# RWKV-7 preparation in a hybrid decoder block: TensorE order written out, head sums as 64x64 products, bias one-hot loaded earlier

## The chip, the cores and the metric

One core of one Trainium2 chip. TensorE multiplies, VectorE and ScalarE do the elementwise work (ScalarE also the functions that need a table, such as Ln, Exp and Tanh), GpSimd (POOL in the profile) does a little of both, and SyncE, ScalarE and GpSimd issue DMAs. The metric is the device time of one execution in microseconds; several executions are given by their median.

## The reference

One decoder block on a sequence of 512 positions and 1024 channels, float32. The normed input is projected once; the columns go to a sparse-attention mixer (8 query heads, 2 key groups), an RWKV-7 mixer (8 heads of 64) and two gates. The two mixers are projected, gated, merged, projected again and added to the input; a gated MLP with a short convolution follows. The part that matters here is the preparation of the RWKV recurrence and the bias table of the attention:

```python
xl = p_in + (shifted - p_in) * mu
r, k, v, xw, xa, xg = jnp.split(xl, RWKV_SPLITS, axis=-1)
w = -jax.nn.softplus(-(w0 + jnp.tanh(xw) @ w2)) - 0.5
decay = jnp.exp(-jnp.exp(w.astype(jnp.float32)))
a = jax.nn.sigmoid(a0 + xa @ a2)
...
kk = k * k_k.reshape(H, N).astype(jnp.float32)
kk = kk / jnp.maximum(jnp.sqrt(jnp.sum(kk * kk, axis=-1, keepdims=True)), 1e-12)
k = k * (1.0 + (a - 1.0) * k_a.reshape(H, N).astype(jnp.float32))
...
y = y + jnp.sum(r * k * r_k, axis=-1, keepdims=True) * v
```

Two of these lines hold a sum over the 64 channels of each head: the norm of kk, and the bonus r * k * r_k.

## The kernel before, in words

Activations lie with channels on the 128 partitions and the 512 positions along the free dimension, so that one tile of 128x512 holds a *pair* of heads (64 partitions each). There are NH2 = 4 pairs. The weights are streamed as tiles of 128x1024 float32 (`raw`, 3 buffers); ScalarE rounds each to `whi` and VectorE (for a few tiles GpSimd) takes the rest `wlo` (line 296, 2 buffers each). The rounded input is `hh`, its rest `hl`. A *dense block* (`dense_fm`) is 24 products of 128x128 weights over 512 columns into one PSUM bank: for each of 8 k-tiles whi x hh and whi x hl, then 8 times wlo x hh.

PSUM has 8 banks, in three rings: `mm` with 4 banks, `a` with 2 and `b` with 2 (`mmb()`, `pa()`, `pb()`). A bank that is asked for again must first have been read by whoever reads its last contents.

The stage in question, lines 478 to 610, does for each pair p:

- `front(p)`: the dense block of the keys, two products of 64 rows with `wa` for decay and a (ring a and ring b), the shift mix of the keys (`shift_mix`, line 441: a copy with a scale on ScalarE, then a multiply-add on VectorE), two tanh, the cumulative sum over each chunk of 64 positions (`cum`, line 506), the exponentials `ep` and `pi`, and `PC` (line 513), the last decay of each chunk.
- `norms(p)`: the square of the keys, the *head sum* of it, that is a product with the block-diagonal 128x128 matrix `ones` (part of the tile `kc`) over 512 columns, then max (VectorE), Ln and Exp (ScalarE) into `rn`. Ln and Exp lie in different tables, so ScalarE loads a table ahead of each.
- `receptance(p)` and `values_of(p)`: a dense block and a shift mix each (`rx`, `vx`). `vx` has one buffer.
- `values_tok(p)`: four transposes of `vx` (line 542), copied to `UV` by ScalarE.
- `vectors(p)`: the elementwise products on VectorE that make `AR`, `kk`, `bh`, `aa`, `kx` and `tv`; at its end the head sum of `tv` and `BO`, the bonus.
- `gram(p)`: 16 transposes of `bh` (line 573, products of 64 rows, two at a time) into a bank of ring b and one of ring a, their copy `BKT` on ScalarE, then 16 products of 64x128 of `bh` with `AR`, the first half into rings b and a, the second into ring mm, and their masked copies `AB` on VectorE.

The loop stands at line 589. It names the steps in an order, but the order on each engine is the scheduler's. On TensorE it came out, for a steady pair, as: v block of p, k block of p + 1, the wa products, the value transposes of p, then the r block of p + 1 with the head sums of kk (p + 1) and tv (p) inside it, then transposes and products of the gram of p. So the small products of a pair lie in three places.

After the stage VectorE inverts 32x32 triangles (`inv`, memset on GpSimd at lines 620 and 621, transposes at 625 and 730) while TensorE runs the q block (`dense_tok`) and others, until `below` (line 740) needs the inverse. The bias table of the attention is one product of `rel_bias` (with a row of a large negative number) with a one-hot matrix. Both are loaded by ScalarE's DMA queue (lines 698 and 699) into a part of the tile `QK`; that part is also where the squares of q are written, so the loads come after these.

Of the kernel before, what the change touches and what calls it, by code (L numbers as in the profile page):

```python
# [25 lines left out]
NH2 = H // 2  # L26
# [54 lines left out]
def hybrid_block(ctx: ExitStack, tc: tile.TileContext, A: dict, out: bass.AP):  # L81
# [31 lines left out]
    def pa():  # L113
        return bank("a", 2)
# [376 lines left out]

    def front(p):
        cs = slice(128 * p, 128 * p + 128)
        kx = t2("kx", 2)
        pk = dense_fm(hh, hl)
        zw, za = pa(), pb()
        mm(zw, wa[0:64, cs], xw[0:64], True, True)
        mm(za, wa[64:128, cs], xw[64:128], True, True)
        shift_mix(pk, 4 + p, kx)
        cl = t2("cl")  # L500
# [12 lines left out]
        v.tensor_copy(PC[:, p, :, None], ep[:, :, C:C + 1])  # L513
        L[p] = dict(kx=kx, aa=aa, ep=ep, pi=pi)

    def norms(p):
        kx = L[p]["kx"]
        kk = t2("kk", 2)
        act(kk, kx, AF.Square, scale=col("rwkv_k_k", p))
        ss = pa()  # L520
        mm(ss, ones, kk, True, True)
        rn = t2("rn", 2)
        ts(rn, ss, 1e-24, None, op0=ALU.max)
        act(rn, rn, AF.Ln)
        act(rn, rn, AF.Exp, scale=-0.5)
        L[p].update(kk=kk, rn=rn)

# [20 lines left out]
    def vectors(p):  # L548
# [12 lines left out]
        stt(tv, rx, col("rwkv_r_k", p), kx, ALU.mult, ALU.mult)  # L561
        L[p]["bh"] = bh
        bs = pa()
        mm(bs, ones, tv, True, True)
        tt(BO[:, p], bs, vx, ALU.mult)

    def gram(p):
        bh = L[p]["bh"]
        ptr = [pb(), pa()]
        for c in range(NCH):  # L570
            for r in range(2):
                rs = slice(64 * r, 64 * r + 64)
                te.transpose(ptr[r][:, 64 * c:64 * c + 64], bh[rs, c, r:r + 2].rearrange("p a t -> p (a t)"),
                             ident[rs, rs])
        for r in range(2):
            act(BKT[:, :, p, r, :], ptr[r].rearrange("p (c j) -> p c j", c=NCH))
        for c0 in range(0, NCH, 4):
            ptr = [mmb(), mmb()] if c0 else [pb(), pa()]
            for i in range(4):
                for r in range(2):  # L580
                    rs = slice(64 * r, 64 * r + 64)
                    mm(ptr[r][:, 128 * i:128 * i + 128], bh[rs, c0 + i, r:r + 2].rearrange("p a t -> p (a t)"),
                       AR[rs, p, c0 + i].rearrange("p a t -> p (a t)"), True, True)
            for r in range(2):
                tt(AB[:, c0:c0 + 4, p, r, :], ptr[r].rearrange("p (c t) -> p c t", c=4),
                   mask[:, None, :].to_broadcast([128, 4, 128]), ALU.mult)


    front(0)
    norms(0)  # L590
    receptance(0)
    values_of(0)
    late_params()
    for p in range(NH2):
        if p + 1 < NH2:
            front(p + 1)
            norms(p + 1)
        values_tok(p)
        vectors(p)
        if p + 1 < NH2:  # L600
            receptance(p + 1)
        gram(p)
        if p + 1 < NH2:
            values_of(p + 1)
        if p + 2 == NH2:
            kcp = dense_fm(hh, hl)
    dbg("AR", AR)
# [72 lines left out]
    def windows(a, p):  # L680
        for g in range(2):
            for r in range(2):
                act(Dc[64 * r:64 * r + 64, a, g, :], p[64 * g:64 * g + 64, r::2])

    windows(0, kcp)
    urgent.append(1)
    bq = dense_tok(512, hh, hl)
    for t in range(NT):
        act(qn[:, t], bq[t])
        for h in range(H):  # L690
            act(QK[:, 2048 + 64 * h:2112 + 64 * h], bq[t][:, 64 * h:64 * h + 64], AF.Square,
                accum_out=qss[:, t, h:h + 1])
    windows(1, dense_fm(hh, hl))


    oh, rbx, vb = QK[0:33, 2048:2432], QK[0:33, 2440:2448], QK[0:8, 2560:2944]
    nc.gpsimd.memset(rbx[32:33], NEG)
    sc.dma_start(rbx[0:32], A["rel_bias"])
    sc.dma_start(oh, A["onehot"])
    pt = pa()  # L700
# [681 lines left out]
```

## Time and profile before

| | |
|---|---|
| median of 3 runs | 843.86 us (843.79 to 844.13) |
| the profiled execution's own time | 844.05 us |
| its span, first to last instruction | 842.3 us |
| mean granted TensorE clock | 1.0 |
| TensorE busy | 829.1 us, 98% |
| VectorE, ScalarE, GpSimd busy | 514.0, 405.9 and 52.4 us |

The page gives busy time by engine, then the span in slices, the DMA queues, the chain that ended last, and the groups of instructions. In a row of the timeline stand the start and the duration in us, the engine, the line, the operation, out<-in by tile name, the shape and the count; square brackets hold the idle time before it and who ended that. PE is TensorE, DVE is VectorE, ACT is ScalarE, POOL is GpSimd; q behind a name is the engine's own issuing of DMAs. TensorE's products are pipelined: the next starts before the row before has ended, so that the distance between starts is what one costs. The RWKV stage runs from about 27 to 123 us of the span.

### The profile page before, as it was taken

The page shows a single profiled execution, that of the slowest core. Times are in us where ns is not written, and L with a number is a line of the kernel's source. Part 1 is how long each engine was busy: PE and PEld are TensorE (multiplying, and loading weights), DVE is VectorE, ACT ScalarE, POOL GpSimd, SP SyncE. Part 2 cuts the span into 40 slices and gives each one's busy share as a digit, 9 for nine tenths or more (in the row PEclk, how much of TensorE's full clock was granted, in tenths as well). Part 3 has the DMA queues.
Part 4 walks back from the last instruction along what each step waited for, and adds up shares of the span by engine and source line. Part 5 has one row for each costly group of instructions (what it writes and reads, how often), then busy time and mean ns, then how long its engine had stood idle before and what let it go on. Part 6 is the DMA issues. An engine that isn't in the chain of part 4 may idle for free.

```text
span 842.3 us, 12845 instructions
## 1 busy us (share of the span) xinstructions
PE 829.1 (98%) x5097; PEld 674.3 (80%) x5097; DVE 514.0 (61%) x998; ACT 405.9 (48%) x784; POOL 52.4 (6%) x69
## 2 busy tenths in 40 slices
PE   7999999999999999999999999999999999999998
PEld 6777778887787886777788988888888888888886
DVE  5477779963556678888675576666556666322222
ACT  6766655452545677677344454444444444221210
POOL 6200020140000110111000000000000000000000
PEclk9999999999999999999999999999999999999999
DMA  7432222335461320010167033333333332223421
GB/s 228 115 82 68 75 75 76 92 104 156 126 126 51 88 63 13 22 31 26 51 204 234 0 99 90 90 97 100 100 100 100 96 90 93 98 100 113 138 75 51
DMA packets 109104, 78.73 MB, mean 93 GB/s; under 512 B 3869, under 2 KB 97748, under 8 KB 109044
## 3 DMA queue, kind: packets, MB, share of 16 engines
q1 hardware_dynamic: 106512, 73.51, 30.0%
q0 software_dynamic: 1472, 1.86, 1.0%
q10 hardware_dynamic: 1060, 2.55, 1.0%
q8 instruction: 40, 0.66, 0.3%
q14 instruction: 20, 0.16, 0.1%
HBM read 74.56 MB, written 2.29 MB: 91 GB/s over the span
## 4 chain that ended last, share of the span: by engine, by line
PE 53%; DVE 0%; DVEq 0%; issue 0%
PE ps_mm L120 52%; PE ps_b L203 0%; PE ps_a L203 0%; PE ps_a L120 0%; PE ps_b L1186 0%; PE ps_mm L1186 0%; DVE x L126 0%; DVEq L1378 0%; PE ps_a L1138 0%
## 5 line engine op out<-in xcount | busy, mean ns | idle before, releaser
L296 DVE TENSOR_TENSOR wlo<-raw,whi 128x1024 fp32r<-128x1024 f32 (+1 forms) x111 | 131.5, 1186 | 187.2 <-PE ps_mm L120 158.8
L120 PE MATMUL ps_mm<-hh,whi 128*128 128x512 f32 (+1 forms) x624 | 242.6, 391 | 0.0
L120 PE MATMUL ps_mm<-hl,whi 128*128 128x512 f32 (+1 forms) x624 | 240.4, 387 | 0.0
L123 ACT ACTIVATE whi<-raw 128x1024 fp32r<-128x1024 f32 (+3 forms) x124 | 123.3, 996 | 171.1 <-PE ps_mm L120 143.0
L120 PE MATMUL ps_mm<-hh,wlo 128*128 128x512 f32 (+1 forms) x624 | 151.8, 384 | 0.0
L120 PEld LDWEIGHTS ps_mm<-hh,whi 128*128 128x128 f32 x624 | 117.3, 188 | 26.7 <-issue 1.3
L120 PEld LDWEIGHTS ps_mm<-hl,whi 128*128 128x128 f32 x624 | 117.4, 188 | 23.5 <-issue 1.0
L120 PEld LDWEIGHTS ps_mm<-hh,wlo 128*128 128x128 f32 x624 | 115.1, 188 | 23.4
L120 PE MATMUL ps_mm<-whi,aT 128*128 128x512 f32 x352 | 84.5, 390 | 0.0
L120 PEld LDWEIGHTS ps_mm<-whi,aT 128*128 128x128 f32 x352 | 65.9, 188 | 14.3 <-issue 0.4
L135 DVE SCALAR_TENSOR_TENSOR cgv<-ps_mm,cw,cgv 128x511 f32<-128x511 f32 (+1 forms) x88 | 65.4, 746 | 1.6
L123 ACT ACTIVATE cgv<-ps_mm,cw 128x512 f32<-128x512 f32 x44 | 34.3, 781 | 23.3 <-PE ps_mm L120 23.3
L120 PE MATMUL ps_mm<-wlo,aT 128*128 128x512 f32 x176 | 44.3, 389 | 0.0
L123 ACT ACTIVATE P<-P,nm 128x512 f32<-128x512 f32 (+3 forms) x64 | 35.4, 553 | 14.9 <-DVE nm L1160 14.9
L123 ACT ACTIVATE aT<-cgv 128x512 fp32r<-128x512 f32 x22 | 13.9, 632 | 56.8 <-DVE cgv L126 56.8
L120 PEld LDWEIGHTS ps_mm<-wlo,aT 128*128 128x128 f32 x176 | 33.0, 188 | 6.9
L123 ACT ACTIVATE cgv<-cgv 128x512 f32<-128x512 f32 x22 | 13.9, 632 | 41.0 <-DVE cgv L135 41.0
L296 POOL TENSOR_TENSOR wlo<-raw,whi 128x512 fp32r<-128x512 f32 (+3 forms) x13 | 20.4, 1569 | 203.9 <-PE ps_mm L120 148.1
L1160 DVE CUSTOM_DVE_ANT_0 P<-ps_a,AB 128x512 f32<-128x512 f32 (+3 forms) x64 | 29.4, 484 | 4.2 <-PE ps_a L120 3.7
L126 DVE TENSOR_TENSOR x<-x,ps_mm 128x512 f32<-128x512 f32 (+1 forms) x17 | 11.0, 654 | 22.6 <-PE ps_mm L120 20.2
L126 DVE TENSOR_TENSOR aT<-cgv,aT 128x512 fp32r<-128x512 f32 x22 | 15.2, 693 | 14.7 <-ACT aT L123 14.7
L120 PE MATMUL ps_a<-KH,qst 128*128 128x512 f32 (+3 forms) x64 | 21.3, 348 | 1.5 <-DVE nm L1160 0.9
(356 smaller groups left out, 1201.7 us busy)
## 6 DMA issues: line engine op xcount, KB each, us to landing
raw<-in_w_up_dram SPq DMA_DIRECT2D x44, 512.0 KB, 3.8
raw<-in_w_in_dram SPq DMA_DIRECT2D x38, 512.0 KB, 3.9
raw<-in_w_down_dram SPq DMA_DIRECT2D x22, 512.0 KB, 3.6
raw<-in_w_out_dram SPq DMA_DIRECT2D x8, 512.0 KB, 3.9
xt<-in_x_dram SPq DMA_DIRECT2D x4, 512.0 KB, 5.8
raw<-in_cmp_w_k_dram SPq DMA_DIRECT2D x4, 512.0 KB, 4.4
raw<-in_cmp_w_v_dram SPq DMA_DIRECT2D x4, 512.0 KB, 4.4
raw<-in_w_proj_b_dram SPq DMA_DIRECT2D x8, 256.0 KB, 2.7
```

The lines of the kernel that those rows point to most:

```text
L120: te.matmul(o, lhsT=l, rhs=r, start=start, stop=stop)
L123: sc.activation(o, i, f, **kw)
L126: v.tensor_tensor(o, a, b, op=op)
L135: v.scalar_tensor_tensor(o, a, s, b, op0=op0, op1=op1)
L296: eng.tensor_tensor(lo, raw, hi.bitcast(F32), op=ALU.subtract)
L1160: v.tensor_tensor_reduce(out=P[:, i], in0=sp[:, N * (i - i0):N * (i - i0) + N], in1=BT[:, h, 384 - 128 * qt:512], scale=-1.0, scalar=-NEG, ...
```

## The change

- `front` is split: `keys_of` (k block, shift mix, square) and `decays` (wa products and what follows them).
- `head_sums` replaces each 128x128 product over 512 columns by four products of 64x64 weights over 256 columns: the first 256 columns by the two diagonal quarters into ring a, the other 256 by the two quarters off the diagonal into ring b, where the heads' results come out with their halves exchanged. What reads them (`EXCH`) works on one piece of 128x256 and two of 64x256; the max is in two pieces.
- The head sum of `tv` and `BO` move from the end of `vectors` to a step of their own, `bonus`, behind `gram`.
- `gram` puts its transposes into two banks of ring mm and its first products too, the second half into rings b and a (in the last pair the other way round); the copies to `BKT` have a high priority.
- TensorE's order is the written one for the whole stage: per pair the v block (at the end of the step before), the k block, the value transposes, the r block, then wa, head sum of kk, transposes and products of the gram, and the bonus sum in one stretch.
- The memset and the two loads for the bias table go to GpSimd's DMA queue, ahead of the q block; the squares of q are written in place in PSUM.

The scheduler still orders the other engines. In the changed program, for a steady pair, VectorE has: wlo of the next k block, mix of rx, the two max, cl, the scan, two AB, PC, AR, two AB, three BO, kk, AR, kk, bh, aa, the copy of bh, kx, wlo, mix of vx, the second part of bh, tv, wlo, mix of kx. ScalarE has: rx, the two tanh, a table load, Ln, two BKT, a table load, ep, pi, three Exp for rn, whi, vx, whi, kx, four UV, the square, whi. On GpSimd's queue the order is: the first memset of the inverse's tile, the bias memset, the load of rel_bias, the spare wlo (a part of the q weights that GpSimd splits), the second memset of the inverse's tile, the load of the one-hot.

```diff
--- before.py
+++ after.py
@@ -489,14 +489,18 @@
     L = {}
 
 
-    def front(p):
+    def keys_of(p):
+        kx = t2("kx", 2)
+        shift_mix(dense_fm(hh, hl), 4 + p, kx)
+        kk = t2("kk", 2)
+        act(kk, kx, AF.Square, scale=col("rwkv_k_k", p))
+        L.setdefault(p, {}).update(kx=kx, kk=kk)
+
+    def decays(p):
         cs = slice(128 * p, 128 * p + 128)
-        kx = t2("kx", 2)
-        pk = dense_fm(hh, hl)
         zw, za = pa(), pb()
         mm(zw, wa[0:64, cs], xw[0:64], True, True)
         mm(za, wa[64:128, cs], xw[64:128], True, True)
-        shift_mix(pk, 4 + p, kx)
         cl = t2("cl")
         act(cl, zw, AF.Tanh, scale=0.5, bias=w0h[:, p:p + 1])
         aa = t2("aa", 2)
@@ -511,19 +515,31 @@
         pi = t2("pi", 2)
         act(pi, cum, AF.Exp, scale=-1.0)
         v.tensor_copy(PC[:, p, :, None], ep[:, :, C:C + 1])
-        L[p] = dict(kx=kx, aa=aa, ep=ep, pi=pi)
+        L.setdefault(p, {}).update(aa=aa, ep=ep, pi=pi)
+
+
+
+    def head_sums(src):
+        o = [pa(), pb()]
+        for i in range(2):
+            for r in range(2):
+                a, b = slice(64 * r, 64 * r + 64), slice(64 * (r ^ i), 64 * (r ^ i) + 64)
+                mm(o[i][b, 0:256], ones[a, a], src[a, 256 * i:256 * i + 256], True, True)
+        return o
+
+    EXCH = [(slice(0, 128), slice(0, 128), 0), (slice(0, 64), slice(64, 128), 1), (slice(64, 128), slice(0, 64), 1)]
 
     def norms(p):
-        kx = L[p]["kx"]
-        kk = t2("kk", 2)
-        act(kk, kx, AF.Square, scale=col("rwkv_k_k", p))
-        ss = pa()
-        mm(ss, ones, kk, True, True)
+        kk = L[p]["kk"]
+        ss = head_sums(kk)
         rn = t2("rn", 2)
-        ts(rn, ss, 1e-24, None, op0=ALU.max)
-        act(rn, rn, AF.Ln)
-        act(rn, rn, AF.Exp, scale=-0.5)
-        L[p].update(kk=kk, rn=rn)
+        for i in range(2):
+            ts(kk[:, 256 * i:256 * i + 256], ss[i][:, 0:256], 1e-24, None, op0=ALU.max)
+        act(kk, kk, AF.Ln)
+        for d, s_, i in EXCH:
+            cs = slice(256 * i, 256 * i + 256)
+            act(rn[d, cs], kk[s_, cs], AF.Exp, scale=-0.5)
+        L[p]["rn"] = rn
 
     def receptance(p):
         rx = t2("rx", 2)
@@ -559,23 +575,27 @@
         stt(bh[:, :, 1, :], chunks(kx), 1.0, chunks(pi), ALU.mult, ALU.mult)
         tv = t2("tv")
         stt(tv, rx, col("rwkv_r_k", p), kx, ALU.mult, ALU.mult)
-        L[p]["bh"] = bh
-        bs = pa()
-        mm(bs, ones, tv, True, True)
-        tt(BO[:, p], bs, vx, ALU.mult)
+        L[p].update(bh=bh, tv=tv)
+
+    def bonus(p):
+        bs = head_sums(L[p]["tv"])
+        for d, s_, i in EXCH:
+            cs = slice(256 * i, 256 * i + 256)
+            tt(BO[d, p, cs], bs[i][s_, 0:256], L[p]["vx"][d, cs], ALU.mult)
 
     def gram(p):
         bh = L[p]["bh"]
-        ptr = [pb(), pa()]
+        ptr = [mmb(), mmb()]
         for c in range(NCH):
             for r in range(2):
                 rs = slice(64 * r, 64 * r + 64)
                 te.transpose(ptr[r][:, 64 * c:64 * c + 64], bh[rs, c, r:r + 2].rearrange("p a t -> p (a t)"),
                              ident[rs, rs])
-        for r in range(2):
-            act(BKT[:, :, p, r, :], ptr[r].rearrange("p (c j) -> p c j", c=NCH))
+        with tc.high_priority():
+            for r in range(2):
+                act(BKT[:, :, p, r, :], ptr[r].rearrange("p (c j) -> p c j", c=NCH))
         for c0 in range(0, NCH, 4):
-            ptr = [mmb(), mmb()] if c0 else [pb(), pa()]
+            ptr = [pb(), pa()] if c0 or p == NH2 - 1 else [mmb(), mmb()]
             for i in range(4):
                 for r in range(2):
                     rs = slice(64 * r, 64 * r + 64)
@@ -586,24 +606,28 @@
                    mask[:, None, :].to_broadcast([128, 4, 128]), ALU.mult)
 
 
-    front(0)
-    norms(0)
-    receptance(0)
-    values_of(0)
-    late_params()
-    for p in range(NH2):
-        if p + 1 < NH2:
-            front(p + 1)
-            norms(p + 1)
-        values_tok(p)
-        vectors(p)
-        if p + 1 < NH2:
-            receptance(p + 1)
-        gram(p)
-        if p + 1 < NH2:
-            values_of(p + 1)
-        if p + 2 == NH2:
-            kcp = dense_fm(hh, hl)
+    with tc.manual_schedule(engines={mybir.EngineType.PE}):
+        keys_of(0)
+        decays(0)
+        receptance(0)
+        norms(0)
+        values_of(0)
+        late_params()
+        for p in range(NH2):
+            vectors(p)
+            if p + 1 < NH2:
+                keys_of(p + 1)
+            values_tok(p)
+            if p + 1 < NH2:
+                receptance(p + 1)
+                decays(p + 1)
+                norms(p + 1)
+            gram(p)
+            bonus(p)
+            if p + 1 < NH2:
+                values_of(p + 1)
+            if p + 2 == NH2:
+                kcp = dense_fm(hh, hl)
     dbg("AR", AR)
     dbg("BO", BO)
     close(tp_cm)
@@ -682,21 +706,21 @@
             for r in range(2):
                 act(Dc[64 * r:64 * r + 64, a, g, :], p[64 * g:64 * g + 64, r::2])
 
+    oh, rbx, vb = QK[0:33, 2048:2432], QK[0:33, 2440:2448], QK[0:8, 2560:2944]
+    nc.gpsimd.memset(rbx[32:33], NEG)
+    nc.gpsimd.dma_start(rbx[0:32], A["rel_bias"])
+    nc.gpsimd.dma_start(oh, A["onehot"])
     windows(0, kcp)
     urgent.append(1)
     bq = dense_tok(512, hh, hl)
     for t in range(NT):
         act(qn[:, t], bq[t])
         for h in range(H):
-            act(QK[:, 2048 + 64 * h:2112 + 64 * h], bq[t][:, 64 * h:64 * h + 64], AF.Square,
-                accum_out=qss[:, t, h:h + 1])
+            hs_ = bq[t][:, 64 * h:64 * h + 64]
+            act(hs_, hs_, AF.Square, accum_out=qss[:, t, h:h + 1])
     windows(1, dense_fm(hh, hl))
 
 
-    oh, rbx, vb = QK[0:33, 2048:2432], QK[0:33, 2440:2448], QK[0:8, 2560:2944]
-    nc.gpsimd.memset(rbx[32:33], NEG)
-    sc.dma_start(rbx[0:32], A["rel_bias"])
-    sc.dma_start(oh, A["onehot"])
     pt = pa()
     mm(pt[0:8, 0:384], rbx, oh, True, True)
     act(vb, pt[0:8, 0:384])
```

## The prediction

> **What bounds the kernel now.** I read the page's busy shares first, then the list of TensorE's waits, then its timeline in the RWKV stage, then ScalarE and VectorE in the same stretch.
>
> ```profile
> PE 829.1 (98%) x5097; PEld 674.3 (80%) x5097; DVE 514.0 (61%) x998; ACT 405.9 (48%) x784; POOL 52.4 (6%) x69
> PE ps_mm L343 <- DVE h L130: 0.5, 1, 0.5
> PE ps_b L542 <- DVE vx L135: 0.3, 1, 0.3
> PE ps_mm L120 <- DVE AB L126: 0.2, 1, 0.2
> ```
>
> TensorE is the bound. In the first 240 us, which hold all that the change touches, only the waits for vx and for AB (0.5 us together) lie in the RWKV stage. So the change can win only through shorter TensorE work, and it loses wherever another engine makes TensorE wait. VectorE and ScalarE have slack as shares, but both stand in a loop with TensorE, so the order of their work decides.
>
> ```profile
> 67.77 0.39 PE L120 MATMUL ps_mm<-hh,whi 128*128 128x512 f32 x1
> 71.40 1.98 PE L120 MATMUL ps_mm<-hh,wlo 128*128 128x512 f32 x8
> 73.31 0.69 PE L120 MATMUL ps_a<-xw,wa 64*128 64x512 f32 x1
> 73.31 0.69 PE L120 MATMUL ps_b<-xw,wa 64*128 64x512 f32 x1
> 74.36 0.66 PE L542 MATMUL ps_b<-kc,vx 128*128 128x128 f32 x4
> 74.78 0.48 PE L120 MATMUL ps_mm<-hh,whi 128*128 128x512 f32 x1
> 76.94 1.02 PE L120 MATMUL ps_a<-kk,kc 128*128 128x512 f32 x2
> 77.80 1.02 PE L120 MATMUL ps_a<-tv,kc 128*128 128x512 f32 x2
> 82.19 0.27 PE L573 MATMUL ps_b<-kc,bh 64*128 64x64 f32 x1
> 84.67 0.50 PE L120 MATMUL ps_mm<-hh,whi 128*128 128x512 f32 x1
> 97.25 0.48 PE L120 MATMUL ps_mm<-hh,whi 128*128 128x512 f32 x1
> ```
>
> Starts, not the modelled ends, give the prices. One dense block: 16 products from 67.77 to 71.40 are 0.227 us each, so its 24 take 5.44. The wa products: 73.31 to 74.36, 1.05. The value transposes: 0.42. A head sum: 76.94 to 77.80, 0.86. Transposes and products of the gram: 82.19 to 84.67, 2.48. The r block of one pair starts at 74.78, that of the next at 97.25: 22.47 a pair.
>
> **The head sums.** Eight of them (kk and tv of four pairs) become four 64x64 products over 256 columns each. Whether four quarters run at once is shown by the recurrence later on:
>
> ```profile
> 200.39 0.22 PE L120 MATMUL ps_b<-Xs,AB 64*64 64x64 f32 x1
> 200.39 0.22 PE L120 MATMUL ps_b<-UV,AB 64*64 64x64 f32 x1
> 200.40 0.22 PE L120 MATMUL ps_b<-Xs,AB 64*64 64x64 f32 x1
> 200.40 0.27 PE L120 MATMUL ps_b<-UV,AB 64*64 64x64 f32 x2
> ```
>
> Four starts within 10 ns. With half the columns at the same rate, a sum costs 0.43 if the quarters run together, 0.86 if two by two, 1.71 if one by one. I take 0.43, as these rows are of the same shape of weights: 8 x 0.43 = 3.4 us less TensorE work, with 0 and -6.8 (a loss) as the other bounds.
>
> Against it stands the changing of tile shapes: a pair now goes from dense to wa (64 rows), head sum (64x64), gram (64 rows), bonus sum (64x64) and back, five changes where there were four. The row: the dense block's eight last products should end at 71.40 + 8 x 0.227 = 73.22 and the wa products start at 73.31, so a change costs about 0.1, 0.1 a pair more. [...]
>
> **The first part, up to the v block of pair 1** (62.20 in the trace). It holds three sums (kk of 0 and 1, tv of 0): 3 x 0.43 = -1.3. Before, kk(0) was also late:
>
> ```profile
> 33.92 0.40 PE L120 MATMUL ps_mm<-hh,whi 128*128 128x512 f32 x1
> 34.46 1.13 PE L120 MATMUL ps_a<-kk,kc 128*128 128x512 f32 x2
> ```
>
> 0.54 between the starts where 0.23 is usual: 0.31 lost. Now a whole dense block lies between the keys and their sum, so this goes: -1.6 in all. Against it the new wait at the v block, next.
>
> **The new waits, in a steady pair.** The fixed order is v block, k block of the next pair, value transposes, r block, then wa, head sum, transposes, gram, bonus sum in one stretch. Let R be the end of the r block. TensorE itself is through the stretch at R + 1.05 + 0.43 + 2.48 + 0.43 + 0.1 = R + 4.5. But the v block's bank is the one in which the first transposes lay, and ScalarE must have copied it (BKT). In the new ScalarE order a table load and Ln stand ahead of BKT, and the load waits for VectorE's two max operations on the head sum; these stand behind wlo and the rx mix, and wlo waits for the end of the r block.
>
> ```profile
> 79.33 1.28 ACT L123 ACT_TABLE_LOAD   x1
> 80.62 0.63 ACT L123 ACTIVATE rn<-rn 128x512 f32<-128x512 f32 x1
> 81.16 1.04 ACT L123 ACTIVATE whi<-raw 128x1024 fp32r<-128x1024 f32 x1
> 84.75 0.59 ACT L123 ACTIVATE BKT<-ps_b 128x512 f32<-128x512 f32 x1
> 85.23 0.60 ACT L123 ACTIVATE BKT<-ps_a 128x512 f32<-128x512 f32 x1
> 82.36 1.22 DVE L296 TENSOR_TENSOR wlo<-raw,whi 128x1024 fp32r<-128x1024 f32 x1 [2.81 <-PE ps_mm L120]
> 84.89 0.75 DVE L135 SCALAR_TENSOR_TENSOR rx<-ps_mm,prm,rx 128x511 f32<-128x511 f32 x1 [1.31 <-ACT rx L123]
> 85.56 0.74 DVE L135 SCALAR_TENSOR_TENSOR kk<-kx,prm,rn 128x512 f32<-128x512 f32 x1
> 86.22 0.69 DVE L135 SCALAR_TENSOR_TENSOR AR<-rx,ep 128x512 f32<-128x512 f32 x1
> 88.62 1.28 DVE L126 TENSOR_TENSOR AB<-ps_mm,kc 128x512 f32<-128x512 f32 x2
> 92.90 0.69 DVE L135 SCALAR_TENSOR_TENSOR bh<-kx,pi 128x512 f32<-128x512 f32 x1
> 94.17 1.22 DVE L296 TENSOR_TENSOR wlo<-raw,whi 128x1024 fp32r<-128x1024 f32 x1
> 95.31 0.74 DVE L135 SCALAR_TENSOR_TENSOR vx<-ps_mm,prm,vx 128x511 f32<-128x511 f32 x1
> 95.96 1.22 DVE L296 TENSOR_TENSOR wlo<-raw,whi 128x1024 fp32r<-128x1024 f32 x1
> ```
>
> wlo started 0.17 after the r block's end (82.19) and takes 1.14 (94.17 to 95.31); the mix takes 0.67 (84.89 to 85.56). The two max operations on 256 columns have no row: half of a 512-column operation is 0.35, a whole one 0.7; I take the half, as their work is halved, 0.7 together. The load starts at R + 2.7, Ln 1.29 later, BKT 0.54 after that, 0.6 long, with 0.1 of passing on: R + 5.2. The v block waits 0.7.
>
> Next, what this makes late. The second BKT (0.48 later), the second table load and ep (0.63) put PC, which needs ep and stands in VectorE's order ahead of nearly everything, at R + 7.6. Behind it: PC 0.2, two AR (1.2), kk (0.66), bonus in three pieces (no row; 3 x 0.33 = 1.0 by half width, 1.8 by full), and of the run from 88.62 to 95.96 (7.34) all but bh's second half and tv (1.27), which come after vx now: 6.1. Sum 9.2. vx is ready at R + 16.8. TensorE has ended the k block at R + 5.2 + 2 x 5.44 = R + 16.1 and waits 0.7 for it; then 0.42 for the transposes, 5.44 for the r block and 0.3 for three changes: the next R is R + 23.0. Against 22.47: **+0.5 a pair**, over two pairs +1.0. The loop is through ScalarE and VectorE, so the cheaper sums cannot show in it.
>
> **The last pair and after.** Saved: its tv sum 0.43 and the two waits of before (0.5 together). New: the value transposes wait 0.7 again, and the bonus sum waits for a bank until a mask product of the gram is done, about 0.2: together 0. Behind the stage, the bias table:
>
> ```profile
> 152.54 0.28 PE L120 MATMUL ps_mm<-spare,hh 128*128 128x256 f32 x1
> 152.75 0.81 PE L120 MATMUL ps_a<-QK 33*8 33x384 f32 x2
> 163.04 4.46 DVE L730 STREAM_TRANSPOSE sg<-inv 32x1024 f32<-32x1024 f32 x2
> 168.74 0.21 PE L120 MATMUL ps_a<-sg,AB 32*32 32x32 f32 x1
> ```
>
> The one-hot product starts 0.21 after its neighbour, 0.1 more than the 0.12 by which those follow each other: its DMAs had no wait to give back, so moving them and the memset to GpSimd's queue wins 0 (at most 0.1). On that queue the bias memset and the first load's issue now stand ahead of the spare wlo and the inverse's second memset; what covers that is that the spare part is one of the last of the q block to be used and that the inverse waits for the last AB anyway. Without that cover it would cost the two issues. The squares written in place keep their number and size.
>
> Sum: -1.6 + 0.7 + 0.1 for switches + 1.0 + 0 = **+0.2**, against the profiled execution's 844.05 (span 842.3): 844.25. That execution lay 0.19 above the median of the runs shown, so 844.1.
>
> **The rivals.**
> *A, the waits do not come.* If ScalarE and VectorE run ahead of what I added up (0.7 us in each of the two chains suffices), TensorE's own work decides: -3.4 - 0.3 + 0.4 for switches = -3.3, 840.6; with half of the waits 842.3. For it: the smaller pieces may cost less than half. Against it: the chains are sums of measured rows in a fixed order.
> *B, the quarters do not run together.* Two by two, the stretch ends at R + 5.4 instead of 4.5, mostly under the BKT wait, and the three sums of the first part lose 1.3: about 845.4. One by one: 850. Against it: the four rows at 200.39.
> *C, VectorE becomes the bound (the other side).* If the narrow operations cost as much as whole ones, max +0.7 and bonus +0.8 stand in the loop: +1.5 for each of two pairs, +0.5 in the last: 847.6. It passes 0.2% from +0.75 a pair. The inverse chain behind the stage ends 0 to 1.2 us ahead of its use (163.04 + 4.46 = 167.50 against 168.74), and a slip beyond that is lost too. Against it: nothing but the estimate of halves.
> *D, the change does not do what it says*: the sums get cheaper off the path, the small products are still two stretches a pair, the one-hot was never late: 844, inside the forecast.
> *E, each table load has as long a pause beside it as it lasts itself.* Two loads stand in the loop: +2.6 a pair, 849. The load's end at 79.33 + 1.28 is 0.01 before the next start, so no such pause. [...]
>
> **How the numbers follow.** A change of 0.2% (1.7 us) is about what a measurement of this kernel can tell. Chances: forecast with D 0.42 (843.0 to 845.3), A 0.34, B 0.10, C 0.12, E 0.02. Within 0.2% 0.42, faster 0.34, slower 0.24. The range reaches to A's full gain and most of C: 839.8 to 847.0.
>
> **What would show it.** In the changed profile: r blocks 23.0 apart; 0.7 of waiting before the v block, released by ScalarE's BKT, and before the value transposes, released by VectorE's vx; four quarter products starting together, the next work 0.43 later. Wrong if r blocks stand 21.6 apart (22.47 - 0.86), if the waits are over 1.5, or if the `below` products wait for sg.

## The result, and the profile after

| | before | after |
|---|---|---|
| median of 6 runs each, taken together | 843.87 us (843.79 to 844.13) | 847.27 us (847.16 to 848.96) |
| the profiled execution's own time | 844.05 us | 847.21 us |
| its span | 842.3 us | 845.4 us |

The ratio of the means is 1.0044, 95% interval 1.0034 to 1.0054: 0.44% slower. The forecast was 844.1 us, with a range up to 847.0: the measured time lies 3.2 us above it, and above the range.

The page of the changed kernel opens with busy time by engine; under it stand its waits of TensorE from 28 to 127 us (who waited, for whom, us in total, times, longest):

```profile
PE 826.4 (98%) x5145; PEld 672.5 (80%) x5145; DVE 517.9 (61%) x1010; ACT 410.2 (49%) x792; POOL 53.3 (6%) x71
```

```profile
PE ps_b L558 <- DVE vx L135: 2.5, 3, 0.9
PE ps_mm L592 <- DVE bh L135: 1.6, 1, 1.6
PE ps_mm L120 <- ACT BKT L123: 1.4, 3, 0.5
PE ps_a L120 <- DVE AB L126: 0.5, 1, 0.5
```

TensorE is busy for 2.7 us less and waits for 6.0 us here, where it waited 0.5. Its timeline shows where: the starts of the v blocks, with the first wa product of each pair, the four quarters of one head sum of kk (each is two instructions, 0.26 apart), and the last pair up to the q block.

```profile
56.36 0.69 PE L120 MATMUL ps_a<-xw,wa 64*128 64x512 f32 x1
57.42 0.43 PE L120 MATMUL ps_a<-kk,kc 64*64 64x256 f32 x2
57.43 0.43 PE L120 MATMUL ps_b<-kk,kc 64*64 64x256 f32 x2
57.68 0.38 PE L120 MATMUL ps_a<-kk,kc 64*64 64x256 f32 x2
58.01 0.71 PE L592 MATMUL ps_mm<-kc,bh 64*128 64x64 f32 x16
61.61 0.50 PE L120 MATMUL ps_mm<-hh,whi 128*128 128x512 f32 x1 [0.46 <-ACT BKT L123]
79.70 0.69 PE L120 MATMUL ps_a<-xw,wa 64*128 64x512 f32 x1
84.96 0.50 PE L120 MATMUL ps_mm<-hh,whi 128*128 128x512 f32 x1 [0.46 <-ACT BKT L123]
96.99 0.66 PE L558 MATMUL ps_b<-kc,vx 128*128 128x128 f32 x4 [0.84 <-DVE vx L135]
103.05 0.69 PE L120 MATMUL ps_a<-xw,wa 64*128 64x512 f32 x1
108.30 0.50 PE L120 MATMUL ps_mm<-hh,whi 128*128 128x512 f32 x1 [0.45 <-ACT BKT L123]
120.34 0.66 PE L558 MATMUL ps_b<-kc,vx 128*128 128x128 f32 x4 [0.86 <-DVE vx L135]
122.56 0.71 PE L592 MATMUL ps_mm<-kc,bh 64*128 64x64 f32 x16 [1.57 <-DVE bh L135]
125.60 0.43 PE L120 MATMUL ps_a<-tv,kc 64*64 64x256 f32 x2 [0.48 <-DVE AB L126]
126.19 0.50 PE L120 MATMUL ps_mm<-whi,hh 128*128 128x512 f32 x1
```

For the last pair before the change, three rows: the value transposes, the q block, and GpSimd's split.

```profile
118.58 0.66 PE L542 MATMUL ps_b<-kc,vx 128*128 128x128 f32 x4 [0.26 <-DVE vx L135]
122.86 0.50 PE L120 MATMUL ps_mm<-whi,hh 128*128 128x512 f32 x1
118.47 2.35 POOL L296 TENSOR_TENSOR wlo<-raw,whi 128x1024 fp32r<-128x1024 f32 x1 [90.84 <-PE ps_mm L120]
```

So the 3.1 us of span divide as follows. Up to the v block of pair 1: 61.61 against 62.20, -0.6. Each of the two steady pairs: 84.96 - 61.61 = 23.35 against 22.47, +0.88, together +1.76. From the last v block to the q block: 126.19 - 108.30 = 17.89; before it was 122.86 - 107.15 (62.20 and two pairs of 22.47), 15.71: +2.18. That makes +3.3 at the q block (126.19 against 122.86), of which the rest of the program gives 0.2 back.

What happens in the last pair is on VectorE and GpSimd. VectorE's rows, then GpSimd's:

```profile
119.54 0.74 DVE L135 SCALAR_TENSOR_TENSOR vx<-ps_mm,prm,vx 128x511 f32<-128x511 f32 x1
120.20 2.31 DVE L135 SCALAR_TENSOR_TENSOR bh<-kx,pi 128x512 f32<-128x512 f32 x1
```

```profile
119.62 2.34 POOL L296 TENSOR_TENSOR wlo<-raw,whi 128x1024 fp32r<-128x1024 f32 x1 [91.71 <-DVE wlo L296]
```

The second part of bh costs 0.68 elsewhere; here it lasts 2.31 and ends at 122.51, after GpSimd's split of a q weight (until 121.96). The gram's transposes need it and wait 1.57. Before, the split ran at about the same time, from 118.47 to 120.82, but bh and tv were done at 116.7 and VectorE had nothing to do from 118.5 on, until the bonus product's result came at 120.13:

```profile
115.98 0.74 DVE L135 SCALAR_TENSOR_TENSOR tv<-rx,prm,kx 128x512 f32<-128x512 f32 x1
120.13 0.69 DVE L126 TENSOR_TENSOR BO<-ps_a,vx 128x512 f32<-128x512 f32 x1 [1.61 <-PE ps_a L120]
```

And the steady pair, on ScalarE and then on VectorE:

```profile
82.49 1.28 ACT L123 ACT_TABLE_LOAD   x1 [0.36 <-DVE kk L130]
83.79 0.63 ACT L123 ACTIVATE kk<-kk 128x512 f32<-128x512 f32 x1
```

```profile
82.00 0.41 DVE L130 TENSOR_SCALAR kk<-ps_b 128x256 f32<-128x256 f32 x1
87.37 0.17 DVE L517 COPY PC<-ep 128x8 f32<-128x8 f32 x1 [2.18 <-ACT ep L123]
88.65 0.68 DVE L126 TENSOR_TENSOR AB<-ps_a,kc 128x512 f32<-128x512 f32 x1
89.25 0.42 DVE L126 TENSOR_TENSOR BO<-ps_a,vx 128x256 f32<-128x256 f32 x1
89.68 0.86 DVE L126 TENSOR_TENSOR BO<-ps_b,vx 64x256 f32<-64x256 f32 x2
90.57 0.75 DVE L135 SCALAR_TENSOR_TENSOR kk<-kx,prm,rn 128x512 f32<-128x512 f32 x1
96.19 0.74 DVE L135 SCALAR_TENSOR_TENSOR vx<-ps_mm,prm,vx 128x511 f32<-128x511 f32 x1
```

The load waits for the two max, as forecast, and the chain from PC to vx is a gapless run of VectorE from 87.37 to 96.93. Its three pieces of BO take 1.32, where a whole operation of the same kind takes 0.60 (AB, 88.65 to 89.25).

### The profile page after: what moved, and what is told of

It is laid out like the page before. It is cut to its first block, busy times and chain, and to the rows that moved or that the text cites. A ratio compares the mean times of both kernels' runs of the same rounds, so it can differ in the third digit from the quotient of the medians.

```text
span 845.4 us, 12966 instructions
## 1 busy us (share of the span) xinstructions
PE 826.4 (98%) x5145; PEld 672.5 (80%) x5145; DVE 517.9 (61%) x1010; ACT 410.2 (49%) x792; POOL 53.3 (6%) x71
## 4 chain that ended last, share of the span: by engine, by line
PE 53%; DVE 0%; DVEq 0%; issue 0%
PE ps_mm L120 52%; PE ps_a L203 0%; PE ps_b L203 0%; PE ps_a L120 0%; PE ps_b L1210 0%; PE ps_mm L1210 0%; DVE x L126 0%; DVEq L1402 0%; PE ps_a L1162 0%
## 5 line engine op out<-in xcount | busy, mean ns | idle before, releaser
L120 PE MATMUL ps_mm<-whi,hh 128*128 128x280 f32 (+2 forms) x72 | 22.6, 334 | 0.3 <-ACT QK L123 0.3
```

The costliest lines, as they stand in the source:

```text
L120: te.matmul(o, lhsT=l, rhs=r, start=start, stop=stop)
```

## The experiments

Ratios are to the kernel before, run on the same chip at the same time. Its medians there lie between 843.97 and 844.26, against 843.87 above, so times of runs made at different times compare to about 0.4 us; distances within a trace are finer.

**Which half of the change costs: the order or the quarters?** First the new order with every head sum a whole product again.

```diff
-        ss = head_sums(kk)
+        ss = pa()
+        mm(ss, ones, kk, True, True)
...
-        bs = head_sums(L[p]["tv"])
+        bs = pa()
+        mm(bs, ones, L[p]["tv"], True, True)
```

> The changed kernel with its head sums as whole 128x512 products again (max, Exp and BO as one 512-column operation each); order and loads stay changed. Theory (a loop through VectorE sets the pair): BO costs VectorE 1.32 us in three pieces (89.25 to 90.57) and 0.66 whole, so vx comes 0.7 earlier, while TensorE's stretch grows by 2 x 0.3 to R + 5.2, where BKT stands anyway. A pair takes 22.7 instead of 23.35; the first part loses about 0.5, the last pair gains 0.5: about 1.3 us faster than the changed kernel, near 846. Rival (TensorE's own work decides): eight sums at 0.3 more each, 2.4 us slower, near 849.6.

843.4 us, ratio 0.9990 [0.9981, 0.9999]: 3.9 faster than the changed kernel, where about 1.3 was expected. Its list of waits in this stretch; then from its timeline GpSimd's split and VectorE's bh in the last pair, and the table load of a steady pair:

```profile
PE ps_a L120 <- DVE AB L126: 0.2, 1, 0.2
```

```profile
118.11 2.85 POOL L296 TENSOR_TENSOR wlo<-raw,whi 128x1024 fp32r<-128x1024 f32 x1 [90.16 <-DVE bh L135]
117.39 0.68 DVE L135 SCALAR_TENSOR_TENSOR bh<-kx,pi 128x512 f32<-128x512 f32 x1
81.27 1.28 ACT L123 ACT_TABLE_LOAD   x1
```

Neither the wait for vx, nor the one for BKT, nor the one for bh is left; a pair takes 22.54 (wa products at 56.28, 78.83 and 101.31). bh comes just ahead of the split. The table load starts 2.44 after the first wa product (81.27 - 78.83) and not 2.79 (82.49 - 79.70): in the program of the changed kernel the load ahead of Ln carries the wait for the max, which come as two operations; with one max the load carries none. So the order alone is no loss but 0.8 us faster (843.4 against 844.24 beside it), and the whole loss, and that 0.8, is in the quarters.

Then the quarters in the kernel before, with its own order (`head_sums` and the split max, Exp and BO alone).

```diff
-        ss = pa()
-        mm(ss, ones, kk, True, True)
+        ss = head_sums(kk)
...
-        bs = pa()
-        mm(bs, ones, tv, True, True)
+        bs = head_sums(tv)
```

> The kernel before with the head sums as quarters alone; TensorE's order is the scheduler's, the bank rings and the loads are as before. Theory (the order is what costs, the quarters save TensorE work where VectorE has slack): a sum costs 0.55 (57.42 to 58.01 in the changed kernel) instead of 0.86, 8 x 0.3 = 2.4 us faster, 841.4; if changing shapes inside a dense block costs 0.1 each way, 1.0 faster, 842.9. Rival (the narrow BO and Exp cost as much as they save): 844 to 845.

850.61 us, ratio 1.0074 [1.0061, 1.0086]: slower than both expected. The largest of the waits, and ScalarE before the gram of one pair:

```profile
PE ps_b L120 <- ACT UV L123: 4.2, 3, 1.4
```

```profile
83.69 1.28 ACT L123 ACT_TABLE_LOAD   x1
84.98 1.27 ACT L123 ACTIVATE rn<-kk 128x256 f32<-128x256 f32 x3
86.28 0.77 ACT L123 ACTIVATE UV<-ps_b 64x256 f32<-64x256 f32 x2
```

The quarters need a bank of ring b as well. In the old order the gram's products then get the bank in which the value transposes lay, and ScalarE copies the last of that (UV, 86.28) only behind a table load and Exp. So the quarters could not come without new rings for the gram.

The third part, the one-hot loads and the memset on GpSimd's queue (and the squares of q in place), with the rest as before:

```diff
+    nc.gpsimd.memset(rbx[32:33], NEG)
+    nc.gpsimd.dma_start(rbx[0:32], A["rel_bias"])
+    nc.gpsimd.dma_start(oh, A["onehot"])
     windows(0, kcp)
...
-    sc.dma_start(rbx[0:32], A["rel_bias"])
-    sc.dma_start(oh, A["onehot"])
```

> The kernel before with the bias memset and loads on GpSimd's queue ahead of the q block and the squares in place, nothing else. Theory: nothing waited for them, 843.9 within 0.3. Rival: the loads on GpSimd's queue hold up the spare wlo or the inverse's memset and cost over 0.5; or they were late and save 0.1 to 0.5.

844.27 us, ratio 1.0000 [0.9991, 1.0009]: no effect, as forecast.

**Is it GpSimd's split that holds bh?** The second tile of the q weights split by VectorE:

```diff
-        yield from rows(w_in, O_Q, 512, eng=[v, pool_, ("spare", pool_), v])
+        yield from rows(w_in, O_Q, 512, eng=[v, v, ("spare", pool_), v])
```

> The changed kernel with the wlo of the second q tile on VectorE instead of GpSimd. Theory: bh's second half of the last pair took 2.31 us instead of 0.68 because GpSimd's wlo (119.62 to 121.96) held it; without that it takes 0.68, the transposes of the last pair wait 0.2 instead of 1.57, and the kernel is 1.4 us faster, near 845.8. Rival (it was held by something else in the last pair, a late operand or ScalarE's copies): it stays at about 2.3 and the time at 847.2 or above.

845.77 us, ratio 1.0018 [1.0009, 1.0027]. bh is back to its length and the gram's transposes wait for nothing. The first two of TensorE's three waits (the third is 0.2 for AB), and the row of bh:

```profile
PE ps_b L558 <- DVE vx L135: 2.6, 3, 0.9
PE ps_mm L120 <- ACT BKT L123: 1.4, 3, 0.5
```

```profile
120.34 0.68 DVE L135 SCALAR_TENSOR_TENSOR bh<-kx,pi 128x512 f32<-128x512 f32 x1
```

About 1.5 us of the loss are the meeting of bh with the split: from the value transposes to those of the gram it takes 0.60 here (120.48 to 121.08) and 2.22 in the changed kernel (120.34 to 122.56). The waits for vx and BKT stay as they were.

**Which of the two sums?** Only kk in quarters:

```diff
-        bs = head_sums(L[p]["tv"])
+        bs = pa()
+        mm(bs, ones, L[p]["tv"], True, True)
```

> The changed kernel with only the kk sum as quarters (two max, three Exp); the tv sum and BO are whole. In this program the table load ahead of Ln carries the wait for the two max, as in the changed kernel. Theory (two additive costs on the loop: the load that waits 0.35 for the max, and BO in three pieces 0.66): only the load's cost is left. From the r block's end PC comes at 7.67 as in the changed kernel, vx at 16.5; TensorE waits 0.2 to 0.3 for vx and a pair takes 22.65 (22.54 with whole sums, 23.35 in the changed kernel); in all about 843.3, or 844.7 if GpSimd's wlo holds up bh in the last pair again. Rival (BO's pieces are not what costs): a pair stays at 23.3, 846 or more.

844.24 us, ratio 1.0001 [0.9992, 1.0010], between the two. A pair takes 22.62, and the load waits here too (81.86, 2.78 after the first wa product). The list of waits has none for vx or BKT, but the starts show them. The last eight products of a k block, and the value transposes behind them:

```profile
93.52 1.98 PE L120 MATMUL ps_mm<-hh,wlo 128*128 128x512 f32 x8
95.63 0.66 PE L558 MATMUL ps_b<-kc,vx 128*128 128x128 f32 x4
```

That is 2.11, where it is 1.82 with whole sums (93.50 to 95.32): TensorE waits 0.29 for vx, which ends at 95.57. The list counts a wait only from the modelled end of a product, so it misses this one. In the same way the v block starts 0.23 late behind BKT (from the tv sum to that block's last eight products 4.87, with whole sums 4.64). In the last pair tv is now the operation beside the split, and the bonus sum waits 1.1 for AB:

```profile
118.28 2.75 POOL L296 TENSOR_TENSOR wlo<-raw,whi 128x1024 fp32r<-128x1024 f32 x1 [90.23 <-DVE vx L135]
118.72 2.85 DVE L135 SCALAR_TENSOR_TENSOR tv<-rx,prm,kx 128x512 f32<-128x512 f32 x1
```

Only tv in quarters:

```diff
-        ss = head_sums(kk)
+        ss = pa()
+        mm(ss, ones, kk, True, True)
```

> The changed kernel with only the tv sum as quarters (BO in three pieces); the kk sum, max and Exp are whole, so the load does not wait. Theory: PC at 7.3 after the r block's end as with whole sums, BO 0.66 longer, vx at 16.8 while TensorE could take it at 16.0: a wait of 0.8 for vx, a pair takes 22.95; 844.2 in all, or 845.7 if bh is held up in the last pair. Rival (the load alone is the cost): no wait for vx, a pair at 22.25 and 842.2.

846.93 us, ratio 1.0033 [1.0020, 1.0045]: four fifths of the loss (2.7 of 3.4 us), more than both expected. A pair takes 23.02 (79.39 to 102.41) with three waits for vx (1.8 together), and bh meets the split:

```profile
118.92 2.34 POOL L296 TENSOR_TENSOR wlo<-raw,whi 128x1024 fp32r<-128x1024 f32 x1 [91.59 <-PE ps_mm L120]
119.22 2.60 DVE L135 SCALAR_TENSOR_TENSOR bh<-kx,pi 128x512 f32<-128x512 f32 x1
```

So BO in three pieces makes VectorE late enough to show (23.02 - 22.54 = +0.48 a pair) and moves bh into the split. There the load does not wait (81.84, 2.45 after the first wa product at 79.39). The kk sum in quarters, and with it the load's wait of 0.35, costs 0.08 a pair alone and 23.35 - 23.02 = 0.33 on top of BO.

By the starts the three distances come out of the 22.54. From its start to the gram's transposes a kk sum takes 0.60 in quarters (80.13 to 80.73 with kk alone) and 1.05 whole (79.89 to 80.94), so the quarters save TensorE 0.45; those of tv save 0.28 (4.36 to the v block's last eight products, not 4.64). With kk alone 22.54 - 0.45 + 0.23 + 0.29 = 22.61 (measured 22.62); with tv alone 22.54 - 0.28 + 0.72 of waiting for vx = 22.98 (23.02); with both 22.54 - 0.73 + 0.53 for BKT + 1.00 for vx = 23.34 (23.35). In the changed kernel TensorE thus saves 0.7 a pair and waits 1.5.

**Can the quarters win, if the other engines' orders are written out too?** First VectorE's: PC and the max ahead of the masks, vx ahead of the second part of bh, and the second q split on VectorE.

```diff
-    with tc.manual_schedule(engines={mybir.EngineType.PE}):
+    with tc.manual_schedule(engines={mybir.EngineType.PE, mybir.EngineType.DVE}):
...
+            vec_a(p)
+            values_of(p)
+            vec_b(p)
```

> The changed kernel with all sums as quarters, VectorE's order in the stage written out too (PC and the max ahead of AB, then BO, AR, kk, AR, kk, the wlo and mix of vx, and bh, aa, kx and tv only after it), and the wlo of the second q tile on VectorE. Theory (quarters save TensorE 0.3 each, the loss is all in the queue order of VectorE and ScalarE): BKT is copied ahead of the table loads, vx is ready at 14 after the r block's end, TensorE waits for nothing in a steady pair, which takes 21.6 to 21.9; 8 x 0.3 under the kernel with whole sums (843.4), so 841.0 to 841.6. Rival (the quarters' cost lies in themselves, e.g. shape changes on TensorE): a pair at 22.5 or more and 843.4 or above.

845.30 us, ratio 1.0012 [1.0003, 1.0021]. The waits for vx are gone, and others came: VectorE reaches the max late, so that the banks of the kk sum come free late for the tv sum (3 times 0.6), and the products for the parameters, behind the first kk sum, wait 1.1 (until 40.16).

Then all three engines' orders, with the kk sum first behind the r block, ahead of wa (the second q split stays on VectorE from here on, but for one run):

```diff
+    with tc.manual_schedule(engines={mybir.EngineType.PE, mybir.EngineType.DVE, mybir.EngineType.Activation}):
...
+                norms_a(p + 1)
+                decays_a(p + 1)
+            gram_t(p)
...
+                decays_b(p + 1)
             gram(p)
...
+                norms_b(p + 1)
```

> All eight sums as quarters, with TensorE's, VectorE's and ScalarE's orders in the stage written out: the kk sum first behind the r block, its two max at once, BKT ahead of ep, pi, Ln and the loads, the wlo and mix of vx ahead of bh; the wlo of the second q tile on VectorE. Theory (a quarter sum saves TensorE 0.27 to 0.3 wherever nothing waits in a queue): no waits in a steady pair, R block to R block 21.9; the last pair still waits 0.8 for AB, which stands behind two wlo; 1.3 to 2 us under the kernel with whole sums (843.4): 841.5 to 842.3. Rival (quarters give nothing on TensorE): 843.4 or above.

847.31 us, ratio 1.0044 [1.0031, 1.0056], as slow as the changed kernel. TensorE waits four times, 3.6 together, for whi of the next block, which ScalarE has behind Ln, the loads and Exp (and in the profiled execution the granted clock was 0.57 from 47.5 to 51.5, behind the first of these waits, see the last section). The same with whole sums (the edit of the first run):

```diff
-        ss = head_sums(kk)
+        ss = pa()
+        mm(ss, ones, kk, True, True)
...
```

> The same three written orders with all sums whole (max, Exp and BO one operation each). Theory: TensorE's work is all that counts in a steady pair, so the distance to the quarters is 8 x 0.27 to 0.3, 2.2 to 2.4 us slower than they: 843.7 to 844.6, a pair 22.5. Rival (the quarters' saving is eaten by shape changes or by VectorE): the two are within 0.5.

843.11 us, ratio 0.9991 [0.9982, 1.0000]: a pair takes 22.14 to 22.17, 0.4 less than with VectorE's and ScalarE's orders left open (22.54), and there is no wait for whi. The 0.4 is not these engines' doing, as TensorE waited for nothing in a steady pair there either. Most of it is the new place of the kk sum, behind the r block, whose products have the shape of a whole sum: the sum, the wa products and the gram's transposes now take 2.41 (78.37 to 80.78) where they took 2.66 (78.83 to 81.49). The orders are sound with whole sums; with quarters TensorE is at the next block before whi. So, with quarters again, whi moved ahead of the loads:

```diff
+                v_dense(p + 1)
                 norms_b(p + 1)
```

> As the run with all orders written and all sums as quarters, but the whi of the next k tile stands ahead of the two table loads on ScalarE and its wlo ahead of AR on VectorE: there the k block waited for that whi (1.49 and 0.66 us), which stood behind Ln, both loads and Exp. Theory (the quarters themselves save 0.27 each): no wait in a steady pair, which takes 21.6 instead of 22.14 with whole sums, and 841.0 to 841.6 in all. Rival (quarters don't pay even so): 843 or above.

845.52 us, ratio 1.0017 [1.0008, 1.0027]: 1.8 better, but still slower than the kernel before. Now the first products of the gram wait for the bank that VectorE's mix of rx reads (three times, 1.7 together), and that mix stands behind wlo; the last pair's waits for bh and AB are 2.3. To see the split's price once more, the same with the second q split back on GpSimd:

```diff
-        yield from rows(w_in, O_Q, 512, eng=[v, v, ("spare", pool_), v])
+        yield from rows(w_in, O_Q, 512, eng=[v, pool_, ("spare", pool_), v])
```

> The same with the wlo of the second q tile on GpSimd again. Theory: one of VectorE's operations of bh, kx or tv in the last pair takes 2 us or more while GpSimd's wlo runs and AB is late by about as much as with both wlo on VectorE: within 0.6 of the former run. Rival (bh and tv are done before GpSimd's wlo starts): no such operation, no wait for AB, 0.8 to 1.1 faster.

847.07 us, 1.5 more, where at most 0.6 was expected. bh takes 2.71 beside the split again and the transposes wait 2.7, but the bonus sum no longer waits for AB, so that all waits together grow by 0.4 only. The rest goes with the granted clock, which was 0.79 and then 0.65 behind that wait (121.5 to 127): the one execution with a mean granted clock of 1.0 took 845.99, 0.5 more, as expected. Then the split on VectorE again, and the mix of rx, the max and the scan ahead of wlo:

```diff
+                split = receptance(p + 1)
                 norms_a(p + 1)
                 decays_a(p + 1)
+                split()
```

> As the run with whi early, all sums as quarters, but behind the r block the mix of rx, the two max and the scan stand ahead of the wlo of the next v tile on VectorE (and the copy of rx ahead of its whi on ScalarE). There the first products of the gram waited 0.48 to 0.75 for the bank that the mix of rx reads, since a wlo of 1.14 stood ahead of it. In those two traces a whole kk sum takes 0.96 from the r block's end to the wa products and quarters 0.68. Theory (0.28 a sum, once no queue makes TensorE wait): a steady pair takes 21.6 (22.14 with whole sums), the last pair still loses about 1 to bh and AB, 841.2 to 842.0 in all. Rival (the work left on VectorE makes a new wait again): a pair at 22.1 or more, 843 or above.

844.03 us, ratio 0.9997 [0.9988, 1.0006]: a pair takes 21.63, as expected, with no wait left in it. The rest of the gain is lost in the first pair, where TensorE waits 1.13 (until 39.84) for whi, and in the last, where it waits 2.2 for bh and AB (about 1 was expected).

Last, the first pair's whi ahead of rx again (its wlo in the usual place):

```diff
-        split = receptance(0)
+        rx = t2("rx", 2)
+        shift_mix(dense_fm(hh, hl), 0, rx)
+        L[0]["rx"] = rx
         norms_a(0)
-        split()
```

> As the last run (all orders written, all sums as quarters, the mix of rx ahead of wlo), but in the first pair the whi of the v tile stands ahead of the copy of rx again, so that the first v block does not wait 1.13 for it. Theory: that 1.13 comes off whole: 1.1 under the last run, 0.998 to 0.999 of the kernel before, 842.3 to 843.0. Rival (the loop of the first pair through rn and vx takes it back, or the last pair's waits for bh and AB grow): under 0.5 off.

842.55 us (841.94 to 842.83), ratio 0.9981 [0.9972, 0.9990]: a little faster than both kernels. TensorE's waits from 28 to 127 us, and the kk sum of a steady pair from its first quarter to the first wa product behind it:

```profile
PE ps_a L120 <- DVE AB L126: 1.6, 1, 1.6
PE ps_mm L619 <- DVE bh L135: 0.6, 1, 0.6
PE ps_mm L120 <- ACT QK L123: 0.3, 1, 0.3
```

```profile
77.94 0.43 PE L120 MATMUL ps_a<-kk,kc 64*64 64x256 f32 x2
78.53 0.69 PE L120 MATMUL ps_a<-xw,wa 64*128 64x512 f32 x1
```

A sum with the change of shape behind it takes 0.59 (77.94 to 78.53) here, and one ahead of it 0.1 more (77.94 - 76.72 - 5 x 0.227; the price that the prediction took from the wa products); a whole sum with the change behind it took 0.96 with the same orders (78.37 to 79.33). So a quarter sum is worth about 0.27, not 0.43 (the 0.45 for kk above was against a whole sum that had a change of shape on both sides). The waits of the last pair (2.2 for bh and AB) are still there. This kernel differs from the changed one by more than its orders: its second q split is on VectorE too. And the quarters are only part of its gain. The run with written orders and whole sums had 843.11 us (0.9991), so the quarters, with three more edits of the orders, add 0.56, with intervals that overlap, though a steady pair is 0.5 shorter with them (21.63 against 22.15). Whole sums with those three edits were not run.

## Why the prediction was wrong

*The first part.* Forecast -1.6 + 0.7: the v block of pair 1 at 62.20 - 0.9 = 61.3; measured 61.61. The quarters ran together, the late kk(0) is gone, and the BKT wait came, 0.46 of 0.7. With 0.27 for each of three sums the same working gives -0.8 - 0.3 + 0.46 = -0.65; measured -0.59. The sums were mis-sized, by 0.16 each.

*The steady pair.* Forecast +0.5, measured +0.88. The mechanism was the right one, step by step, from R = 79.70: the load waits for the max, BKT releases the v block at R + 5.26 (forecast 5.2), PC stands at R + 7.67 (7.6), vx is the next wait (0.84 in the list and 1.0 by the starts, forecast 0.7). That ScalarE loads a table ahead of both Ln and Exp is what these programs do (82.49 and 85.41, 1.28 each); no run shows that it must. The term that was off is VectorE's run from PC to the end of vx, 9.56 instead of 9.2, and of that 0.32 is BO: 0.44 a piece (89.25 to 90.57 for three), not "3 x 0.33 = 1.0 by half width". As this run is in the loop, the 0.36 is in the distance, and TensorE's cheaper sums are not. For the max the half-width price held: 0.33 each (81.67, 82.00, 82.33 in the same list of VectorE).

*The last pair: the step that failed.* "New: the value transposes wait 0.7 again, and the bonus sum waits for a bank until a mask product of the gram is done, about 0.2: together 0." It cost 2.18: vx 0.86 against 0.26 (+0.6), the transposes' wait for bh 1.57 (new), the bonus sum's wait for AB 0.48 against 0.2 (+0.3), less 0.3 for the sum. I had written myself that the second part of bh comes after vx now, but costed it at nothing, as in a steady pair the r block covers it. In the last pair there is no r block: the gram's transposes follow the value transposes at once. That alone costs little, as the run with the split on VectorE shows: bh takes 0.68 there, and the gram's transposes have no wait in the list (about 0.2 by the starts). The cost came from what else runs there, which I did not ask. GpSimd's split of the q weight lies at 119.62 to 121.96, and VectorE's bh, due to begin inside it, ended 0.55 after it; without that meeting the kernel takes 845.77 against 847.27, 1.5 us less. I had looked at GpSimd only for its DMA queue.

What the operations read differs: bh and tv, which read only SBUF tiles (kx and pi, rx and kx), took 2.31, 2.60 and 2.71 (bh) and 2.85 (tv), each beside the split, while the mix of vx, with one operand in PSUM (ps_mm), lay under the split but for its first 0.08 (119.54 to 120.20) and took its usual 0.66. No run shows that this difference is the reason.

*The sum* +0.2 was thus short by 0.3 (first part), 2 x 0.4 (steady pairs, mostly BO) and 2.2 (last pair), 3.3 together; 0.2 came back later, and the 0.1 that it held for switches is in these distances already. That leaves 3.0, and 3.1 - 0.2 = 2.9 was missing.

*The rivals.* A needed the waits to stay away; with the scheduler's orders they came. With the orders written out and the split moved, the steady pair came to the 21.6 that it implies, but by chance: 0.3 of the step from 22.47 came with the written orders and whole sums (22.15) and 0.5 with the quarters, where A has 0.86 for the quarters alone. The time came to 842.55, near its case of half the waits (842.3), as 2.2 of waits are left in the last pair and 0.3 behind it. Rival B is excluded by the four starts within 10 ns (57.42 and 57.43, two each). Rival C gave the direction and, at 847.6, nearly the time, but that was luck, as its reason was another: the max did cost half, only BO did not, and 2.2 of the 3.1 us lie in the last pair, where it put 0.5. D falls with the changed order in the trace; as to the one-hot it was right. E is excluded, Ln following the load's end (82.49 + 1.28) at 83.79.

What is shown by runs: that the order alone is no loss (0.9990), that all of the loss comes with the quarters, most of it with those of tv (1.0033 alone), and that the split on GpSimd makes about 1.5 of it. The steady pair adds up from TensorE's saving and the waits by the starts in three runs (22.62, 23.02 and 23.35). That it is the load's wait and BO's pieces that make these waits is read from the rows of ScalarE and VectorE; the max or BO alone, in pieces with a whole sum, was not tried.

## What to carry to other kernels

A cheaper operation on the engine that bounds can be worth nothing while its readers are cut into more pieces on an engine in the same loop: count the readers' pieces at their own price (0.44 each here against 0.60 for the whole) before counting the saving. Go through the last turn of a loop by itself, with the cover that it lacks, and for every instruction that moves look at what GpSimd does at its new time, not only at its queue. When one engine's order is written by hand and the others' left open, a gain may need those written too: the same quarters went from 0.44% slower to 0.19% faster with nothing but order and the split's engine changed. But run the same orders without the change as well: whole sums reached 0.9991 with fewer edits, so about half of the 0.19% can be the quarters'. And compare starts with a run that does not wait, as a list of waits can miss half a microsecond a pair.

## What was not expected of the hardware

*bh and tv ended only after GpSimd's split.* I would have looked for two operations that both go slower. The rows read as if one waited for the other: beside the split, bh or tv ended 0.54 to 0.56 after the split's end in all four traces that show them meeting it (122.51 against 121.96 in the changed kernel, 121.57 against 121.03 with kk alone in quarters, 121.82 against 121.26 with tv alone, 121.66 against 121.11 with the split back on GpSimd), which is about what one of them costs in a row (0.60, bh at 120.34 to tv at 120.94 with the split on VectorE). So these ends fit VectorE doing nothing for them until the split was over; nothing in the traces shows what holds them. The other way round too: where VectorE was at such an operation already, the split took 2.75 (kk alone in quarters, 0.44 of bh left) and 2.85 (whole sums, 0.54 of tv left) instead of 2.34, longer by 0.41 and 0.51, about the rest of that operation.

*The clock fell after a short wait.* With all orders written out and all sums as quarters, a wait of 1.49 us for whi, behind three small products, ended at 46.57. Columns: stretch, length, busy time (instructions) of PE, PEld, DVE, ACT and POOL, the granted clock, DMA share, GB/s.

```profile
47.50:51.50 4.00, 4.00 (x13) 3.09 (x12) 3.92 (x7) 0.54 (x1) 0.00 (x0) 0.57 0.38 95
51.50:55.50 4.00, 4.00 (x21) 3.34 (x20) 3.93 (x8) 0.69 (x1) 0.00 (x0) 1.00 0.14 40
```

TensorE started 13 instructions in that stretch and 21 in the next one of the same length. From 48.21 to 51.20 the products of the dense block came 0.43 apart, where 0.23 is usual. With the second q split back on GpSimd, a wait of 2.7 was followed by 0.79 (121.5 to 123) and 0.65 (123 to 127). But the changed kernel's wait of 1.57 left the clock of its profiled execution at 1.00 from 119 to 130, and so did one of 1.44 with the quarters in the old order (1.00 from 87 to 91). Nor is it the program alone: the five executions of the first kernel had mean granted clocks from 0.997 (848.88 us) to 1.0 (846.87), and two of the changed kernel's six had 0.998 and 0.997 (848.32 and 848.96). What decides stays open, and no run shows that the wait is the cause. Where the clock was 0.57, seven products took 2.99 (48.21 to 51.20) where seven take 1.6: 1.4 us more, beside the wait of 1.49.
